# Where the MLP norms' sums of squares are taken in a two-layer hybrid trunk: one-column TensorE products, or ScalarE rows of the turned residual

## Chip, cores and metric

The kernel runs on one core of a Trainium2 chip. The metric is the device time of one execution in microseconds (us); the time given is the median of three runs. TensorE is called PE below, VectorE DVE, ScalarE ACT, GpSimd POOL, and the DMA queue's engine SP.

## What is computed

The reference is a trunk of two layers over 512 positions with 1024 channels. Each layer is a token mixer (layer 0 a gated DeltaNet, layer 1 a Conformer convolution), a cross-attention of 4 heads into 256 memory rows, and an MLP with 4096 hidden channels. Each of them stands behind an RMS norm and adds onto the residual; a last RMS norm closes.

```python
def rms_norm(x, g):
    y = x * lax.rsqrt(jnp.mean(x * x, axis=-1, keepdims=True) + 1e-6)
    return y * g

def sq_relu_mlp(h, w_up, w_down):
    return jnp.square(jax.nn.relu(h @ w_up)) @ w_down

for layer in range(2):
    h = h + mixer[layer](rms_norm(h, ...))
    h = h + memory_cross_attention(rms_norm(h, xa_norm[layer]), rms_norm(mem, ...), ...)
    h = h + sq_relu_mlp(rms_norm(h, mlp_norm[layer]), mlp_w_up[layer], mlp_w_down[layer])
return rms_norm(h, final_norm)
```

## The kernel before

The residual is held with its channels on the partitions: 8 tiles of 128 channels by 512 tokens (`hres`, in the trace `h`). Every product is made in split precision: each operand is a high part and a low part, and `mm3` (L338 to L342) issues three matmuls for each pair of tiles, `wh` by `xh`, `wh` by `xl` and `wl` by `xh`. Weights come from memory as `raw`; ACT casts `raw` to `wh` (L317), and DVE, for some POOL, subtracts to get `wl` (the helper `tt`, L75). Both subtractions and many other two-input operations therefore show as L75, and are told apart by their tiles.

A `Norm` object collects a norm. `add` is `parts` and `square`: `parts` makes `xh` (ACT, L425) and `xl` (DVE, L78) from the residual tile times the gain; `square` squares the tile on ACT (L447) and adds it to an accumulator, on POOL for all but the last tile and on DVE for the last. `stat` (L454) turns the accumulator into one number for each token: four matmuls of one column each (L458; each a 128 by 128 piece of the squares times a column of ones, and as the operands are 32-bit floats each shows as two records) into the PSUM bank `ssq`, a square root on ACT (L460, behind the load of the table that holds it) and a reciprocal on DVE (L462). For the MLP, `stat(rb2)` squares that reciprocal once more (L464): the MLP's input is not scaled by the norm's factor at all, and since the squared ReLU turns a factor r into r squared, its output is multiplied by `rb2` when it is taken.

The cross-attention's output projection ends in `o_ev` (L1056), which for each of 8 tiles adds the residual (DVE) and calls `nxt.add`, where `nxt` is the MLP's norm. The seven-product forms of the input (`seven`, L430, called for X_FORMS) need four DVE sums on the tiles `ua` and `ub` and two casts and two subtractions (`x41h`, `x23h`, `x41l`, `x23l`) for each pair of tiles.

`mlp` (L1105) runs through four groups of 1024 hidden channels. A group has four pairs p, each of an even and an odd tile (`up_even`, `up_odd`). Group 0 makes its 8 up-products with 24 matmuls each; after each of these 8, `first_chunk(n)` (L1271) hangs in side work: `stat(rb2)` after product 1; after the products 0, 1, 2 and 3 the turning of the residual of one block of 128 tokens (`turn_in`, for each half of the channels 4 PE transposes into the PSUM bank `rT` and an ACT copy to `y`); the last `seven` after product 0. For each pair, ACT casts the squared ReLU to `bh`, DVE makes `bl`, then the sums for the seven-product form and their splits `s41h`, `s41l`, `s23h`, `s23l`.

The down-projection of a group is made by seven products in the order M1, M5, M6, M3, M7, M2, M4 (`product`, L1201, matmuls at L1220 to L1222). M5 goes into two banks `dnc`; its first half uses the pairs p = 0 and 1, its second half p = 2 and 3, and needs `s41h` and `s41l` of these pairs. `take` (L1224, DVE) multiplies a bank by `rb2` and adds it to `y`. At the end of layer 0, `stat_tokens` (L472) makes the next norm's factor from sums of squares that ACT took with its accumulator (L1253); at the end of layer 1, `early` and `late` (L1228 to L1243) do the same for the last norm, block by block: square with accumulator, square root, reciprocal, two scalings and the DMAs out.

The program is written for a tile scheduler: it gives every tile a buffer in a pool (68 in the pool of 512-wide tiles, 8 PSUM banks), sets the semaphores, and decides from its own estimates the order in which each engine's instructions stand. So a change of a few lines moves others.

Of the kernel before, what the change touches and what calls it, by code (L numbers as in the profile page):

```python
# [10 lines left out]
AF = mybir.ActivationFunctionType  # L11
ALU = mybir.AluOpType
# [6 lines left out]
EPS = 1e-6  # L19
# [19 lines left out]
def tile_trunk(ctx, tc, xT, memT, prm_d, adt_d, bdw_d, tap_d, fin_d, w_ab, w_kq, w_v, w_z, w_dno, w_pw1, w_pw2,  # L39
               w_q, w_k, w_vv, w_o, w_up, w_dn, yT):  # L40
    nc = tc.nc
    pe, act, dve, pool = nc.tensor, nc.scalar, nc.vector, nc.gpsimd
# [9 lines left out]
    def nm(s):  # L52
        cnt[0] += 1
        return f"{s}_{cnt[0]}"

    def slot(dt=F32, s="u", shape=(P, NT)):
        return up.tile(list(shape), dt, tag="u", name=nm(s))
# [7 lines left out]
    def psum(s="ps"):  # L65
        return psp.tile([P, NT], F32, tag="ps", name=nm(s))

    def small(n, s="sm"):
        return sp.tile([P, n], F32, tag="sm", name=nm(s))
# [4 lines left out]
    def tt(e, o, a, b, op):  # L74
        return e.tensor_tensor(out=o, in0=a, in1=b, op=op)  # L75
# [4 lines left out]
    def ts(e, o, a, s1, op0, s2=None, op1=None):  # L80
        if op1 is None:
            e.tensor_scalar(out=o, in0=a, scalar1=s1, scalar2=None, op0=op0)
        else:
            e.tensor_scalar(out=o, in0=a, scalar1=s1, scalar2=s2, op0=op0, op1=op1)

    def c4(t):
        return t.rearrange("p (c i) -> p c i", c=4)

    def over_i(t4, n=P):
        return t4.unsqueeze(2).to_broadcast([P, t4.shape[1], n])  # L90

    def over_c(t, n=4):
        return t.unsqueeze(1).to_broadcast([P, n, t.shape[1]])
# [302 lines left out]
    def diag2(v, n):  # L396

        vh = sp.tile([P, n], F32R, tag="sm", name=nm("vh"))
        dve.tensor_copy(vh, v)
        vl = small(n, "vl")  # L400
        tt(dve, vl, v, vh.bitcast(F32), ALU.subtract)
        r = []
        for x in (vh.bitcast(F32), vl):
            d = slot(F32R, "dg")[:, 0:n * P]
            tt(dve, d.rearrange("p (c i) -> p c i", c=n), over_c(ident, n), over_i(x), ALU.mult)
            r.append(d)
        return r
# [6 lines left out]
    class Norm:  # L414
# [36 lines left out]
            else:  # L451
                tt(dve if self.n == KT else self.eng, self.acc, self.acc, sq, ALU.add)

        def stat(self, squared=None):  # L454
            ps = psum("ssq")
            for c in range(4):
                cs = slice(c * P, (c + 1) * P)
                pe.matmul(ps[:, c:c + 1], self.acc[:, cs], ones[:, 0:1], start=True, stop=True)  # L458
            sd = small(4, "sd")
            act.activation(sd, ps[:, 0:4], AF.Sqrt, bias=eps_rms, scale=1.0 / 1024)  # L460
            self.tok = small(4, "rstd")
            dve.reciprocal(self.tok, sd)  # L462
            if squared is not None:
                tt(dve, squared, self.tok, self.tok, ALU.mult)  # L464
                return
            if self.two:
                self.dg = diag2(self.tok, 4)
                return
            self.dg = slot(s="dg")
            tt(dve, c4(self.dg), over_c(ident), over_i(self.tok), ALU.mult)  # L470
# [19 lines left out]
    def keepc(n, s):  # L490
        return cp.tile([P, n], F32, tag=s, name=s)
# [496 lines left out]
    def xattn(layer, norm, hres, nxt):  # L988
# [67 lines left out]
        def o_ev(m, ps):  # L1056
            hn = slot(s="h")
            if layer == 0:
                tt(dve, by_phase(hn), phased(ps), phased(hres[m]), ALU.add)
            else:  # L1060
                tt(dve, hn, ps, hres[m], ALU.add)
            new.append(hn)
            nxt.add(m, hn)
            for q in range(4):
                if X_FORMS[q] == m - 8:
                    nxt.seven(q, *new[2 * q:2 * q + 2])

        def ow(m):
            return wnext(("xo", layer, m // 2), m % 2), psum("xo")
# [23 lines left out]
        for k in (6, 7):  # L1093
            proj(w0, outs, p0, k, k + 1)
            proj(w1, outs, p1, k, k + 1)
        o_ev(0, p0)
        o_ev(1, p1)
        for m in range(2, 8):
            w, ps = ow(m)
            proj(w, outs, ps)  # L1100
            o_ev(m, ps)
# [2 lines left out]

    def mlp(layer, norm, hres, nxt, mid=None):  # L1105
        xs = norm.xs
        rb2 = keepc(4, f"rb2_{layer}")
        last = layer == 1
        y = [[None] * 2 for _ in range(4)]
        bank, forms, done = {}, {}, {}  # L1110
# [5 lines left out]
        def turn_in(t, half):  # L1116
            ps = psum("rT")
            for j in range(4):
                pe.transpose(ps[:, j * P:(j + 1) * P], hres[4 * half + j][:, t * P:(t + 1) * P], ident)
            y[t][half] = slot(s="y")  # L1120
            act.copy(y[t][half], ps)

        def lows(src, s):
            h, lo = slot(F32R, s + "h"), slot(F32R, s + "l")
            act.copy(h, src)
            tt(dve, lo, src, h.bitcast(F32), ALU.subtract)
            return [(h[:, c], lo[:, c]) for c in (slice(0, 256), slice(256, 512))]
# [141 lines left out]
            nxt.stat_tokens(ss)  # L1269

        def first_chunk(n):  # L1271
            if n == 1:
                norm.stat(rb2)
            for t in range(4):
                if TURN_IN[t] == n:
                    for half in range(2):
                        turn_in(t, half)
            for q in range(4):
                if X_FORMS[q] == n:
                    norm.seven(q, hres[2 * q], hres[2 * q + 1])  # L1280

        new = [None] * 8
        for g in range(4):
            for p in range(4):
                if (g, p) in UP_SEVEN:
                    up_seven(g * 4 + p)
                    continue
                for i in range(2):
                    ps = psum("up")
                    proj(wnext(("up", layer, g * 4 + p), i), xs, ps)  # L1290
                    rest()
                    (up_odd if i else up_even)(p, ps)
                    if g == 0:
                        first_chunk(2 * p + i)
# [39 lines left out]
    def phased(t):  # L1334
        return t.rearrange("p (t s) -> p s t", s=4)

    def by_phase(t):
        return t.rearrange("p (s t) -> p s t", s=4)
# [272 lines left out]
    for gq in range(2):  # L1611
# [17 lines left out]
        n = 0  # L1629
# [52 lines left out]
    h = xattn(0, n1, h, n2)  # L1682
    n3 = Norm("cv_norm", dve)
    h = mlp(0, n2, h, n3, lambda i: mem_gain(1, i - 1) if i else (mem_load(), taps(NTAP)))
    n4 = Norm("xa_norm1")
    h = conformer(n3, h, n4)
    n5 = Norm("mlp_norm1")
    h = xattn(1, n4, h, n5)
    mlp(1, n5, h, None)


# [154 lines left out]
```

## Time and profile before

| | |
|---|---|
| median of three runs | 1486.53 us (1486.28 to 1486.94) |
| the profiled execution's own time | 1486.58 us |
| its span in the trace | 1484.9 us |
| granted PE clock | 0.997 of full speed |
| matmul records, all records of ACT, DVE, POOL | 7852; 1479, 1834, 293 |
| busy time of ACT and POOL | 862.6 us (58%), 335.9 us (23%) |

The profile comes from one execution, and its rows are read like this: start in us, duration in us, engine, line of the kernel, operation, output and inputs, shape, how many in a row; in brackets the idle time of the engine ahead of it and what ended it. Matmuls overlap, so the pace of PE is read from start to start, 0.23 us for a 512-column matmul, and not from the durations. 1.68 us of the execution lie around the span.

### The profile page before, as it was taken

How to read it: one execution, taken by the hardware profiler on the slowest of the kernel's cores; microseconds unless marked ns; L12 is line 12 of the kernel's file. 1: busy time of each engine (PE TensorE's matmuls, PEld its weight loads, DVE VectorE, ACT ScalarE, POOL GpSimd, SP SyncE). 2: the span in 40 equal slices, each digit the busy share in tenths (PEclk: the TensorE clock that was granted, in tenths of full speed). 3: DMA queues.
4: the chain of work that ended last, by engine and by line, in shares of the span. 5: the costliest groups of instructions: out<-in, count | busy, mean ns of one | idle time of the engine just before them, and what ended most of it. 6: DMA issues, size and time to landing. Idle time of an engine off the chain costs nothing. (4 is left out here: it accounts for less than half of the span.)

```text
span 1484.9 us, 21162 instructions
## 1 busy us (share of the span) xinstructions
PE 1465.1 (99%) x7852; PEld 1252.8 (84%) x7852; DVE 1151.9 (78%) x1834; ACT 862.6 (58%) x1479; POOL 335.9 (23%) x293
## 2 busy tenths in 40 slices
PE   9999999999999999999999999999999999999998
PEld 6888888988888888888898888978888888888886
DVE  6898889867555787888879599975547696978787
ACT  6846665655444764646466865364435755646465
POOL 1321120102111302213040357312111304131220
PEclk9999999999999999999999999999999999999999
DMA  5321223552212214142341794643213223231501
GB/s 205 100 86 57 72 86 101 175 179 76 87 66 72 86 38 161 58 138 90 113 159 62 201 241 132 215 155 111 75 43 107 79 85 108 78 128 57 170 29 57
DMA packets 54966, 161.01 MB, mean 108 GB/s; under 512 B 6864, under 2 KB 8656, under 8 KB 54864
## 3 DMA queue, kind: packets, MB, share of 16 engines
q1 hardware_dynamic: 53136, 153.38, 31.4%
q0 software_dynamic: 1728, 6.29, 2.3%
q8 instruction: 62, 1.02, 0.3%
q14 instruction: 40, 0.33, 0.1%
HBM read 156.76 MB, written 2.10 MB: 107 GB/s over the span
## 5 line engine op out<-in xcount | busy, mean ns | idle before, releaser
L317 ACT CAST wh<-raw 128x1024 fp32r<-128x1024 f32 (+1 forms) x340 | 327.3, 975 | 353.3 <-issue 68.1
L75 DVE TENSOR_TENSOR wl<-raw,wh 128x1024 fp32r<-128x1024 f32 (+1 forms) x272 | 320.8, 1190 | 99.8 <-ACT wh L317 98.3
L75 POOL TENSOR_TENSOR wl<-raw,wh 128x1024 fp32r<-128x1024 f32 x68 | 150.2, 2213 | 426.2 <-ACT wh L317 402.9
L340 PE MATMUL up<-xh,wh 128*128 128x512 f32 x320 | 125.4, 392 | 0.0
L341 PE MATMUL up<-xl,wh 128*128 128x512 f32 x320 | 124.9, 390 | 0.5 <-DVE xl L78 0.5
L342 PE MATMUL up<-xh,wl 128*128 128x512 f32 x320 | 124.6, 389 | 0.0
L75 DVE TENSOR_TENSOR raw<-raw,raw 128x512 f32<-128x512 f32 (+1 forms) x120 | 97.6, 825 | 1.3 <-DMA raw<-w_up 0.6
L78 DVE SCALAR_TENSOR_TENSOR ca<-x,prm,ca 128x512 f32<-128x512 f32 x120 | 88.3, 748 | 3.3 <-ACT ca L1431 1.3
L340 PE MATMUL h<-xh,wh 128*128 128x512 f32 x192 | 77.8, 405 | 2.2 <-ACT xh L425 2.2
L341 PE MATMUL h<-xl,wh 128*128 128x512 f32 x192 | 75.9, 395 | 0.1
L342 PE MATMUL h<-xh,wl 128*128 128x512 f32 x192 | 75.8, 395 | 0.0
L341 PEld LDWEIGHTS up<-xl,wh 128*128 128x128 f32 x320 | 60.2, 188 | 12.4 <-DVE xl L78 0.9
L342 PEld LDWEIGHTS up<-xh,wl 128*128 128x128 f32 x320 | 60.1, 188 | 12.5
L75 POOL TENSOR_TENSOR sq<-sq,sq 128x512 f32<-128x512 f32 x24 | 37.4, 1557 | 146.7 <-ACT sq L447 109.1
L340 PEld LDWEIGHTS up<-xh,wh 128*128 128x128 f32 x320 | 60.2, 188 | 11.7
L78 DVE SCALAR_TENSOR_TENSOR cva<-cv,prm,cva 128x512 f32<-128x512 f32 x60 | 49.4, 840 | 12.0 <-POOL cva L75 10.9
L1221 PE MATMUL dnc<-wh,s41l 128*128 128x512 f32 x128 | 50.0, 391 | 0.5 <-DVE s41l L75 0.5
L340 PE MATMUL pw<-xh,wh 128*128 128x512 f32 x128 | 50.2, 392 | 0.0
L340 PE MATMUL q<-xh,wh 128*128 128x512 f32 x128 | 50.1, 392 | 0.0
L341 PE MATMUL xo<-aol,wh 128*128 128x512 f32 x128 | 50.0, 391 | 0.0
L341 PE MATMUL q<-xl,wh 128*128 128x512 f32 x128 | 49.9, 390 | 0.0
L342 PE MATMUL pw<-xh,wl 128*128 128x512 f32 x128 | 49.8, 389 | 0.0
(458 smaller groups left out, 4261.1 us busy)
## 6 DMA issues: line engine op xcount, KB each, us to landing
raw<-w_up SPq DMA_DIRECT2D x64, 512.0 KB, 3.7
raw<-w_dn SPq DMA_DIRECT2D x40, 512.0 KB, 4.5
raw<-w_dn SPq DMA_DIRECT2D x48, 256.0 KB, 3.4
raw<-w_pw SPq DMA_DIRECT2D x24, 512.0 KB, 4.7
raw<-w_kq SPq DMA_DIRECT2D x16, 512.0 KB, 3.9
raw<-w_k SPq DMA_DIRECT2D x16, 512.0 KB, 4.3
raw<-w_vv SPq DMA_DIRECT2D x16, 512.0 KB, 4.5
raw<-w_q SPq DMA_DIRECT2D x16, 512.0 KB, 3.6
```

The lines of the kernel that those rows point to most:

```text
L75: return e.tensor_tensor(out=o, in0=a, in1=b, op=op)
L78: return dve.scalar_tensor_tensor(out=o, in0=a, scalar=s, in1=b, op0=op0, op1=op1)
L317: ins = [act.copy(h_, r), tt(pool if gp else dve, l_, r, h_.bitcast(F32), ALU.subtract)]
L340: pe.matmul(ps, wh, xh, start=first, stop=False)
L341: pe.matmul(ps, wh, xl, start=False, stop=False)
L342: pe.matmul(ps, wl, xh, start=False, stop=last)
L1221: pe.matmul(ps, al[:, cs], w[hf][0][:, s_], start=False, stop=False, skip_group_check=more)
```

## The change

The change touches the norm ahead of each of the two MLPs and nothing else in the source. The cross-attention no longer squares and adds the residual tiles; `stat` loses its `squared` argument, and the MLP doesn't call it. Instead, `turn_in` squares the turned residual right from the PSUM bank on ACT, with the accumulator summing each row of 512 into a column of a new tile `sq8`. A row of the turned bank is a token, so the eight columns hold the two halves of the sum for four blocks of tokens. After the last block (t = 3, product 3), DVE adds the two halves, scales them and adds epsilon, and takes the reciprocal: `rb2` without a square root.

```diff
-        def stat(self, squared=None):
+        def stat(self):
             ps = psum("ssq")
...
             dve.reciprocal(self.tok, sd)
-            if squared is not None:
-                tt(dve, squared, self.tok, self.tok, ALU.mult)
-                return
             if self.two:
...
             new.append(hn)
-            nxt.add(m, hn)
+            nxt.parts(m, hn)
...
-        rb2 = keepc(4, f"rb2_{layer}")
+        rb2, sq8 = keepc(4, f"rb2_{layer}"), keepc(8, f"sq8_{layer}")
...
             act.copy(y[t][half], ps)
+            act.activation(slot(s="fq"), ps, AF.Square, accum_out=sq8[:, 4 * half + t:4 * half + t + 1])
...
         def first_chunk(n):
-            if n == 1:
-                norm.stat(rb2)
             for t in range(4):
                 if TURN_IN[t] == n:
                     for half in range(2):
                         turn_in(t, half)
+                    if t == 3:
+                        tt(dve, rb2, sq8[:, 0:4], sq8[:, 4:8], ALU.add)
+                        ts(dve, rb2, rb2, 1.0 / 1024, ALU.mult, EPS, ALU.add)
+                        dve.reciprocal(rb2, rb2)
```

Counted over the program, for each MLP: PE loses the four `ssq` products (8 records); ACT loses 8 squares from SBUF, the root and one table load and gains 8 squares with accumulator; POOL loses 6 adds; DVE loses one 512-wide add and two operations on 4 columns and gains three such. The number of table loads stays at 26: the root's table is now loaded ahead of the root in `stat_tokens` and, at the end of layer 1, between the first `late` block's square and its root. SP's order is unchanged.

The scheduler also moves instructions that the source doesn't touch. On ACT, in group 0 of layer 0's MLP, the turn-ins of the last two blocks read as follows before (`rT` are the turned banks, `bh` the cast of the second pair):

```order
L1121 COPY y_5097<-rT_5092 128x512
L1121 COPY y_5104<-rT_5099 128x512
L317 CAST wh_5160<-raw_5107 128x1024
L1121 COPY y_5146<-rT_5141 128x512
L1121 COPY y_5153<-rT_5148 128x512
L1144 ACTIVATE up_5106<-up_5106 128x512
L1145 ACTIVATE up_5106<-up_5106 128x512
L1125 CAST bh_5190<-up_5106 128x512
```

And so after the change, on the same engine (three lines less in the source put L1121 at L1118, L1144 at L1142 and L1125 at L1123):

```order
L1118 COPY y_5073<-rT_5068 128x512
L1119 ACTIVATE fq_5075,sq_0_4874<-rT_5068 128x512
L1118 COPY y_5082<-rT_5077 128x512
L1119 ACTIVATE fq_5084,sq_0_4874<-rT_5077 128x512
L1118 COPY y_5126<-rT_5121 128x512
L1119 ACTIVATE fq_5128,sq_0_4874<-rT_5121 128x512
L1118 COPY y_5135<-rT_5130 128x512
L1119 ACTIVATE fq_5137,sq_0_4874<-rT_5130 128x512
L317 CAST wh_5147<-raw_5087 128x1024
L1142 ACTIVATE up_5086<-up_5086 128x512
L1143 ACTIVATE up_5086<-up_5086 128x512
L1123 CAST bh_5177<-up_5086 128x512
```

Four squares now stand ahead of the cast `bh` of the second pair, beside the four of the earlier blocks, and the weight cast has moved behind them.

On DVE, the last pair's `s41l` of the same group, which M5's second half needs, stood before the change as the seventh row here:

```order
L75 TENSOR_TENSOR up_5302<-u_1141_5294,up_5302 128x256
L75 TENSOR_TENSOR wl_5373<-raw_4740,wh_5372 128x1024
L75 TENSOR_TENSOR u_1141_5294<-up_5302,u_1141_5294 128x256
L78 SCALAR_TENSOR_TENSOR y_4948<-dna_5357,rb_0_4896,y_4948 128x512
L75 TENSOR_TENSOR up_5302<-up_5302,u_1141_5294 128x256
L78 SCALAR_TENSOR_TENSOR y_5021<-dna_5364,rb_0_4896,y_5021 128x512
L75 TENSOR_TENSOR s41l_5344<-up_5302,s41h_5343 128x512
```

After the change, the same engine at the same place:

```order
L75 TENSOR_TENSOR wl_5360<-raw_4726,wh_5359 128x1024
L75 TENSOR_TENSOR up_5289<-u_1138_5281,up_5289 128x256
L78 SCALAR_TENSOR_TENSOR y_4926<-dna_5344,rb_0_4873,y_4926 128x512
L75 TENSOR_TENSOR u_1138_5281<-up_5289,u_1138_5281 128x256
L78 SCALAR_TENSOR_TENSOR y_4993<-dna_5351,rb_0_4873,y_4993 128x512
L75 TENSOR_TENSOR up_5289<-up_5289,u_1138_5281 128x256
L75 TENSOR_TENSOR wl_5380<-raw_4781,wh_5379 128x1024
L75 TENSOR_TENSOR wl_5398<-raw_4958,wh_5397 128x1024
L75 TENSOR_TENSOR s41l_5331<-up_5289,s41h_5330 128x512
```

Two 1024-wide subtractions `wl`, which came behind `s41l` before, now stand ahead of it.

On PE, M5's second half (`dnc`) and the beginning of M6 (`dna`, which uses `s23`) stood like this before; the row with `s41l_5344` is the second of the last pair:

```order
L1220 MATMUL dnc_5396<-wh_5351,s41h_5286 128x512
L1221 MATMUL dnc_5396<-wh_5351,s41l_5287 128x512
L1222 MATMUL dnc_5396<-wl_5352,s41h_5286 128x512
L1220 MATMUL dnc_5396<-wh_5351,s41h_5343 128x512
L1221 MATMUL dnc_5396<-wh_5351,s41l_5344 128x512
L1222 MATMUL dnc_5396<-wl_5352,s41h_5343 128x512
```

After the change, on PE from the seventh matmul of M5's second half (the six ahead of it are the third pair's, for both banks):

```order
L1218 MATMUL dna_5344<-wh_5359,s23h_5056 128x512
L1218 MATMUL dnc_5383<-wh_5338,s41h_5330 128x512
L1218 MATMUL dnc_5390<-wh_5338,s41h_5330 128x512
L1219 MATMUL dna_5344<-wh_5359,s23l_5057 128x512
L1220 MATMUL dna_5344<-wl_5360,s23h_5056 128x512
L1218 MATMUL dna_5344<-wh_5359,s23h_5190 128x512
L1219 MATMUL dna_5344<-wh_5359,s23l_5191 128x512
L1220 MATMUL dna_5344<-wl_5360,s23h_5190 128x512
L1219 MATMUL dnc_5383<-wh_5338,s41l_5331 128x512
```

The last pair's `s41l` is wanted after 4 matmuls of this half before, and after 14 now: the third pair's products for the second bank and six matmuls of M6 have moved ahead of it.

## The prediction

> **What bounds the kernel now.** I read the page first, then PE's list of waits, then the timelines of PE, DVE, POOL and ACT around the places that the change touches. The page's line of busy times:
>
> ```profile
> PE 1465.1 (99%) x7852; PEld 1252.8 (84%) x7852; DVE 1151.9 (78%) x1834; ACT 862.6 (58%) x1479; POOL 335.9 (23%) x293
> ```
>
> PE is busy for 99% of the span, so a step matters only where it adds to PE's stream, takes from it, or makes PE wait. Two of PE's waits lie in the two MLPs and can be reached by this change. The first is in layer 0, at the end of the first up-product; PE waits for the last tile's `xl`:
>
> ```profile
> 498.01 0.39 PE L340 MATMUL up<-xh,wh 128*128 128x512 f32 x1
> 498.86 0.50 PE L341 MATMUL up<-xl,wh 128*128 128x512 f32 x1 [0.46 <-DVE xl L78]
> 499.20 0.40 PE L342 MATMUL up<-xh,wl 128*128 128x512 f32 x1
> ```
>
> The matmuls start 0.85 and 0.34 us apart in place of 0.23 each, the pace of such matmuls (rows 1161.19 and 1161.42 below): 0.73 us are lost. The other wait comes in both MLPs, in M5's second half of group 0, where PE wants `s41l` of the last pair:
>
> ```profile
> 550.56 0.39 PE L1222 MATMUL dnc<-wl,s41h 128*128 128x512 f32 x1
> 550.97 0.49 PE L1220 MATMUL dnc<-wh,s41h 128*128 128x512 f32 x1
> 551.69 0.50 PE L1221 MATMUL dnc<-wh,s41l 128*128 128x512 f32 x1 [0.23 <-DVE s41l L75]
> 552.03 0.39 PE L1222 MATMUL dnc<-wl,s41h 128*128 128x512 f32 x1
> ```
>
> ```profile
> 1207.32 0.50 PE L1221 MATMUL dnc<-wh,s41l 128*128 128x512 f32 x1 [0.22 <-DVE s41l L75]
> ```
>
> From 550.56 to 552.03 are 1.47 us for three steps of 0.23, so 0.78 us are lost; layer 1 shows the same wait. This place I call the meeting point: here PE has caught up with the chain ACT to DVE. What PE gains ahead of it is kept only if this chain becomes no later.
>
> **What PE is spared.** The one-column products stand in PE's stream like this, layer 0 and layer 1, each with the transposes behind them:
>
> ```profile
> 505.77 0.95 PE L458 MATMUL ssq<-ones,sq 128*128 128x1 f32 x8
> 506.57 0.42 PE L1119 MATMUL rT<-ident,h 128*128 128x128 f32 x2
> ```
>
> ```profile
> 1161.19 0.39 PE L342 MATMUL up<-xh,wl 128*128 128x512 f32 x1
> 1161.42 0.95 PE L458 MATMUL ssq<-ones,sq 128*128 128x1 f32 x8
> 1162.23 0.64 PE L1119 MATMUL rT<-ident,h 128*128 128x128 f32 x4
> ```
>
> From start to start that is 0.80 and 0.81 us. They go. The wait for `xl` goes too, I think, through POOL. One row of POOL and two of DVE:
>
> ```profile
> 495.77 1.29 POOL L75 TENSOR_TENSOR sq<-sq,sq 128x512 f32<-128x512 f32 x1 [8.64 <-ACT sq L447]
> ```
>
> ```profile
> 495.84 2.31 DVE L75 TENSOR_TENSOR wl<-raw,wh 128x1024 fp32r<-128x1024 f32 x1
> 498.07 0.74 DVE L78 SCALAR_TENSOR_TENSOR xl<-h,prm,xh 128x512 fp32r<-128x512 f32 x1
> ```
>
> POOL's last add of squares ends at 497.06, and the subtraction that DVE began under it takes 2.31 us, where the same operation takes 1.22 alone (the group's mean, quoted below). Without squares to add, POOL isn't there, `wl` ends 1.09 earlier, and `xl` about as much, ahead of the 498.24 at which PE wants it: 0.73 gained. So ahead of the meeting point PE gains 0.80 + 0.73 = 1.53 us in layer 0 and 0.81 in layer 1, 2.34 in all.
>
> **What ACT gets in return.** A square with accumulator is shown elsewhere in the same program, on the same shape, from SBUF:
>
> ```profile
> 1462.13 0.64 ACT L1230 ACTIVATE fq<-y 128x512 f32<-128x512 f32 x1
> 1462.67 0.19 ACT L1230 ACTIVATION_READ_ACCUMULATOR fq<-y 128x1 f32 x1
> 1462.79 0.63 ACT L1230 ACTIVATE fq<-y 128x512 f32<-128x512 f32 x1
> ```
>
> Start to start 0.66 us; if nothing overlapped it would be 0.64 + 0.19 = 0.83. No square from PSUM is shown, so 0.66 to 0.83 are my bounds, and I take 0.66, as the instructions of ACT here also stand close. Eight make 5.3 us, inside the first half of group 0, where ACT leads DVE and DVE leads PE. The squares that go lay in the cross-attention, where ACT waits for residual tiles, and free nothing here. These are ACT's rows of before in that stretch, with POOL's of the same time:
>
> ```profile
> 503.31 0.62 ACT L377 CAST x41h<-ub 128x512 fp32r<-128x512 f32 x1 [2.38 <-DVE ub L75]
> 506.37 1.09 ACT L1121 COPY y<-rT 128x512 f32<-128x512 f32 x2
> 508.56 1.07 ACT L317 CAST wh<-raw 128x1024 fp32r<-128x1024 f32 x1
> 509.65 1.28 ACT L460 ACT_TABLE_LOAD   x1
> 510.94 0.26 ACT L460 ACTIVATE sd<-ssq,eps_rms 128x4 f32<-128x4 f32 x1
> 512.71 0.62 ACT L377 CAST x41h<-ub 128x512 fp32r<-128x512 f32 x1 [1.50 <-DVE rstd L462]
> 513.23 0.58 ACT L1144 ACTIVATE up<-up 128x512 f32<-128x512 f32 x1
> ```
>
> ```profile
> 500.53 2.40 POOL L75 TENSOR_TENSOR wl<-raw,wh 128x1024 fp32r<-128x1024 f32 x1 [3.47 <-PE rT L1119]
> 509.70 2.61 POOL L75 TENSOR_TENSOR wl<-raw,wh 128x1024 fp32r<-128x1024 f32 x1 [6.78 <-ACT wh L317]
> ```
>
> And DVE's, of which the first goes and the second is the sum that `x41h` at 503.31 waits for:
>
> ```profile
> 498.73 0.68 DVE L75 TENSOR_TENSOR sq<-sq,sq 128x512 f32<-128x512 f32 x1
> 500.70 2.51 DVE L75 TENSOR_TENSOR ub<-ub,ua 128x256 f32<-128x256 f32 x1
> ```
>
> Step by step. Without the slow `wl` and the add, DVE starts its four sums 1.7 us earlier; they then end before POOL's `wl` at 500.53, under which the last of them took 2.51 us. So `x41h` comes at about 499.2, four us earlier. ACT can't keep all of that, as it waits for the first pair's `al`; I put the first turn-in copy at 503.7, 2.7 earlier than 506.37. Two squares (1.3) follow, and the cast of 508.56 ends 1.4 earlier. POOL's `wl` of 509.70 waits for this cast, blocks DVE's next sum for its 2.6 us, and now ends 1.4 earlier; `x41h` of 512.71, which needs this sum, is 1.4 earlier. (Its row names `rstd`, since that stood last on DVE ahead of it; the load and `sd` are no longer in ACT's way.) The two activations of the next tile (L1144, L1145), at 0.5 each from start to start, now stand ahead of `x41h` and fill its wait: 1.0 earlier. Then six squares come before the second pair's `bh`: 4.0 later. Together +1.6 us for this row:
>
> ```profile
> 525.42 0.59 ACT L1125 CAST bh<-up 128x512 fp32r<-128x512 f32 x1
> ```
>
> Bounds: without the head start of 1.4 it is +3.0; with 0.83 for each of six squares 1.0 more; at the other end, if all of the 2.7 came through, 1.3 less, +0.3.
>
> `rb2` costs nothing: it's wanted at the first `take`, and on DVE behind its add stands only `bl` of the second pair, which waits for that same `bh`.
>
> **The meeting point.** From that pair's `bl` to `s41l` of the last pair DVE has little slack; the stretch in layer 0 and in layer 1, then two groups of the first:
>
> ```profile
> 526.04:550.95 24.91, 23.53 (x36) 1.00 0.06 21
> 1181.67:1206.59 24.92, 23.54 (x36) 1.00 0.06 22
> ```
>
> ```profile
> L75 DVE TENSOR_TENSOR wl<-raw,wh 128x1024 fp32r<-128x1024 f32 x5 | 6.1, 1220 | 0.4 <-ACT wh L317 0.4
> L75 DVE TENSOR_TENSOR s41l<-up,s41h 128x512 fp32r<-128x512 f32 x3 | 2.1, 688 | 0.7 <-ACT s41h L1125 0.7
> ```
>
> Only 1.38 of 24.91 us are idle, 1.1 of it waiting for ACT (0.7 for `s41h`, 0.4 for `wh`). After the change two more `wl` stand ahead of the last `s41l`. What a pair costs:
>
> ```profile
> 552.15 2.35 DVE L75 TENSOR_TENSOR wl<-raw,wh 128x1024 fp32r<-128x1024 f32 x2
> 554.42 0.74 DVE L78 SCALAR_TENSOR_TENSOR y<-dnc,rb,y 128x512 f32<-128x512 f32 x1
> ```
>
> That is 2.27 us. With `wl` and `raw` work now standing ahead of the `s41l` that waited for ACT, I let the 1.1 us of idle be used up (bounds: none, or all 1.38). The last `s41l` comes 1.6 + 2.3 - 1.1 = 2.8 us later. PE, however, wants it ten matmuls later, 10 x 0.227 = 2.3 us. Net: PE leaves the meeting point 0.5 us later than before, in each MLP, whatever it gained on the way. What it gained it waits: the wait grows from 0.78 lost to about 0.8 + 1.5 + 0.5 = 2.8 in layer 0, and 2.1 in layer 1. Twice 0.5 is +1.0.
>
> **The two moved table loads.** A load now stands ahead of this root, at the end of layer 0:
>
> ```profile
> 828.11 0.28 ACT L475 ACTIVATE sd<-ms,eps_rms 128x4 f32<-128x4 f32 x1
> ```
>
> The root is 1.28 late, but the factor it makes isn't wanted by the next product, which runs on unscaled `xh` tiles made behind it; I take 0.1, bounds 0 and 0.5. The other stands between the first `late` block's square and root, before this row of the last block:
>
> ```profile
> 1478.82 0.63 ACT L1237 ACTIVATE fq<-y 128x512 f32<-128x512 f32 x1 [0.73 <-DVE y L78]
> ```
>
> ACT still waits 0.73 for DVE's `y` in the last block, and waits earlier in the tail too, so most of 1.28 is absorbed; I take 0.2 at the end, bounds 0 and 0.5.
>
> A rule weighed against a row: the load at 509.65 lasts 1.28 and `sd` follows at 510.94, 0.01 us after its end, and the cast ahead of it ends at 509.63. The Trainium skill (ScalarE: Activation LUTs, section What ACT_TABLE_LOAD costs) gives about 1.28 us for the load and a drain of about 1.38 besides, 2.66 for every switch. This trace agrees on the first and shows no drain; by the page's sum the tail's row would be up to 1.4 later, and the estimate for the time 1.4 higher.
>
> **The sum.** The profiled execution took 1486.58 us, 0.05 above the median of 1486.53, so I use it as it is: 1486.58 + 1.0 + 0.1 + 0.2 = **1487.9 us**. About 0.2%, 3.0 us, is what a measurement of this kernel can tell from no change, so faster is below 1483.6 and slower above 1489.5.
>
> **Rivals.**
>
> The cover holds (faster or same). `s41l` comes early enough that PE doesn't lose more than before at the meeting point: 1486.58 - 2.34 + 0.3 = 1484.5; if the wait there vanishes as well, 2 x 0.78 less, 1483.0. For it speaks that ACT is busy only 58% of the whole. Against it: the stretch's 1.38 us of idle can't take two `wl` and a late `bh`. It needs `bh` to be no later than before. Chance 0.14, half of it at 1484.5 (same), half at 1483.0 (faster).
>
> ACT's head start doesn't come (slower). If POOL's `wl` of 509.70 keeps its time, because ACT waits for the first pair's `al` until 506 as before, `bh` is 3.0 late instead of 1.6, and each MLP loses 1.4 more: 1487.9 + 2.8 = 1490.7. For it: layer 1 has no wait for `xl`, so its sums may be less changed than layer 0's. Against: the load and `sd` left ACT either way. It decides from 0.8 us of these 1.4. Chance 0.17.
>
> The load drains (a rule of its own, the skill's of above): a load in the tail keeps ACT 2.66 us, and 1.38 of these come on top, 1489.3. Against it stands the row at 510.94. Chance 0.03.
>
> That the change doesn't do what it says: the wait at 498.86 stays, as `xl` then waits for something else on DVE. It would change nothing, since PE waits at the meeting point anyway; it is inside the forecast.
>
> **How the numbers follow.** The forecast has 0.66 and lies within 0.2%. Faster: 0.07. Slower: 0.17. Same: 0.66 + 0.07 + 0.03 = 0.76. The range goes from 1484.5, the cover that holds but for the old wait, to 1490.7, the missing head start; between them lie the bounds of the single costs (idle not absorbed: 2 x 1.1 more, 1490.1). Outside are the vanished wait, 0.07, and a part of the slower rival where costs add up, about 0.08.
>
> **What would show it.** Right: no `ssq` in either MLP and no wait for `xl` at the first up-product; 0.8 us less between PE's products there; `bh` of the second pair 1.6 us later and `s41l` of the last pair 2.8 later than before; at M5's second half PE loses over 2 us in place of 0.78, in both layers; ACT's squares with accumulator 0.66 apart. Wrong: a meeting point without a longer wait (then the time is below 1485), a `bh` 3 us late, or a wait of PE in a place that has none now, such as the fifth up-product's bank, or the start of layer 1's products behind the moved load.

## The result, and the profile after

The changed kernel takes **1482.65 us** (median of 13 runs, 1481.49 to 1484.39) against 1485.91 us for the kernel before beside it (13 runs, 1485.47 to 1488.48). The medians are 3.26 us apart; the ratio of the runs is 0.9975, with a 95% interval of 0.9967 to 0.9982, that is 2.7 to 4.9 us less. The forecast was 1487.9 us, no difference that can be measured, with a range down to 1484.5; the time lies below it. The profiled execution took 1482.22 us, with a span of 1480.4.

The page's line of busy times after the change:

```profile
PE 1461.6 (99%) x7836; PEld 1250.9 (84%) x7836; DVE 1140.3 (77%) x1834; ACT 862.2 (58%) x1493; POOL 318.0 (21%) x281
```

PE has 3.5 us less to do or to stretch over, POOL 17.9 less, ACT the same: what it gave up and what it took on are alike in sum. Where the time went is read by laying the same matmul of both traces side by side, from place to place; the difference changes at these places only:

| place | PE's difference, after less before |
|---|---|
| start to the first MLP (nothing changed there) | -0.37 us |
| layer 0, last `xl` of the first up-product | -0.74 |
| layer 0, one-column products | -0.78 |
| layer 0, M5's second half, together with M6 | -0.32 |
| layer 1, a wait in the convolution | -0.72 |
| layer 1, one-column products | -0.77 |
| layer 1, M5's second half | -0.67 |
| tail | 0.0 to -0.1 |

The places that the change touches sum to 3.28 us, about the 3.26 between the medians. The first row and the convolution's are matters of the executions that were profiled. For the first row, the granted PE clock is 0.50 over the stretch from 8.0 to 14.6 us in the profile before and over that from 8.7 to 11.9 after, and behind it PE is 1.1 us ahead; a wait of 0.8 us in the mixer, for ACT's `w`, which the profile before doesn't have, takes 0.7 of them back. Other profiles show the same wait at 0.3 to 0.9 us or not at all, before the change and after it. In the convolution PE waits for a row that waits for a weight's transfer. In the kernel before, PE's list of waits, and the row on ACT that came late:

```profile
PE lnT L1499 <- DVE cy L84: 1.2, 1, 1.2
```

```profile
967.35 1.05 ACT L317 CAST wh<-raw 128x1024 fp32r<-128x1024 f32 x1 [0.63 <-DMA raw<-w_vv]
```

After the change this cast follows at once and the wait is 0.5. Of the twelve runs below, one shows 1.5 and the others 0.5, and no row of the convolution stands elsewhere after the change, so I don't count it.

PE at the end of the first up-product of layer 0, and at the end of its second, after the change:

```profile
497.64 0.39 PE L340 MATMUL up<-xh,wh 128*128 128x512 f32 x1
497.86 0.39 PE L341 MATMUL up<-xl,wh 128*128 128x512 f32 x1
498.09 0.40 PE L342 MATMUL up<-xh,wl 128*128 128x512 f32 x1
498.32 1.04 PE L1116 MATMUL rT<-ident,h 128*128 128x128 f32 x8
...
504.45 0.39 PE L342 MATMUL up<-xh,wl 128*128 128x512 f32 x1
504.68 1.03 PE L1116 MATMUL rT<-ident,h 128*128 128x128 f32 x8
```

The matmuls start 0.23 us apart to the last, and the transposes follow the second product with no `ssq` between. Both gains came as forecast. The meeting point did not. PE in M5's second half, layer 0 and then layer 1:

```profile
551.27 0.40 PE L1220 MATMUL dna<-wl,s23h 128*128 128x512 f32 x1
551.76 0.50 PE L1219 MATMUL dnc<-wh,s41l 128*128 128x512 f32 x1
552.10 0.39 PE L1220 MATMUL dnc<-wl,s41h 128*128 128x512 f32 x1
```

```profile
1205.08 0.40 PE L1220 MATMUL dna<-wl,s23h 128*128 128x512 f32 x1
1205.31 0.39 PE L1219 MATMUL dnc<-wh,s41l 128*128 128x512 f32 x1
```

In layer 0, two steps of 0.49 and 0.34 where 0.23 is normal: 0.37 us lost, before 0.78 and by the forecast 2.8. In layer 1 PE meets `s41l` without any wait. The prediction had named this as a sign that it was wrong: a meeting point without a longer wait, with a time below 1485.

### The profile page after: what moved, and what is told of

Same layout as the page of the kernel before. It is cut to its first block, busy times and chain, and to the rows that moved or that the text cites. A ratio compares the mean times of both kernels' runs of the same rounds, so it can differ in the third digit from the quotient of the medians.

```text
span 1480.4 us, 21122 instructions
## 1 busy us (share of the span) xinstructions
PE 1461.6 (99%) x7836; PEld 1250.9 (84%) x7836; DVE 1140.3 (77%) x1834; ACT 862.2 (58%) x1493; POOL 318.0 (21%) x281
## 5 line engine op out<-in xcount | busy, mean ns | idle before, releaser
L342 PE MATMUL q<-xh,wl 128*128 128x512 f32 x128 | 49.9, 390 | 0.0
```

The costliest lines, as they stand in the source:

```text
L342: pe.matmul(ps, wl, xh, start=False, stop=last)
```

## The experiments

Two questions are open: is it the meeting of the chain ACT to DVE with PE at M5 that sets what a step is worth, as the forecast had it, and why was the chain not later? All times are medians; the kernel before had 1486.37 us beside the first four, 1486.31 beside the others. As the kernel before thus differs by up to 0.5 us from set to set (1485.91 beside the changed kernel), a difference of a microsecond between medians of two sets says little; differences by place are read from the profiles, as in the table above.

**No squares.** In `turn_in` the square goes; `sq8` is filled with a constant at the start of `mlp`, so the MLP norm's factor is left out.

```diff
-            act.activation(slot(s="fq"), ps, AF.Square, accum_out=sq8[...])
+        dve.memset(sq8, 512.0)
```

> The changed kernel without its eight squares for each MLP (sq8 is filled with a constant, so the norm's factor in the MLP is left out). Theory 1, the meeting point decides: the chain ACT to DVE and PE come together at M5's second half, and in the changed kernel they meet almost exactly (0.4 us of wait in layer 0, under 0.1 in layer 1). Without squares the chain is about 4 us earlier and nothing but this wait is left to gain: 0.3 to 0.6 us less than the changed kernel, 3.6 to 3.9 less than before. Theory 2, the squares hold up PE or its banks elsewhere in group 0 too: 1.5 us or more less than the changed kernel.

Measured: 1481.46 us, ratio to before 0.9967 (0.9955 to 0.998). By place, 0.5 us less than the changed kernel at M5 in layer 0 and 0.14 in layer 1, and 0.1 or less elsewhere. The eight squares, 4.6 us of ACT in each MLP, cost PE 0.6 to 0.7 us in all.

**Squares twice.**

```diff
             act.activation(slot(s="fq"), ps, AF.Square, accum_out=sq8[...])
+            act.activation(slot(s="fq"), ps, AF.Square, accum_out=sq8[...])
```

> The changed kernel with every square of a turned bank taken twice. Measured price of one square with accumulator from PSUM: 0.58 us from start to start; six more stand ahead of the second pair's bh, 3.5 us. Theory 1, the meeting point decides: PE wants the last s41l only a matmul earlier than in the changed kernel, so each MLP loses 2.5 to 3.5 us there: 5 to 7 us more than the changed kernel, some 2 to 4 slower than before. Theory 2, ACT has slack here (58% busy) and squares are free: within 0.5 us of the changed kernel.

Measured: 1492.35 us, ratio 1.0038 (1.0026 to 1.0051): 9.7 more than the changed kernel. ACT's time isn't free, but the size and the place were missed. PE loses 4.9 us in each MLP, in layer 0 4.1 of them by the first third of the fifth up-product, whose bank was the first pair's odd tile and comes free with its `s41l`. PE at the end of the wait, and then PE's windows, one before it and two behind it:

```profile
521.88 0.50 PE L340 MATMUL up<-xh,wh 128*128 128x512 f32 x1 [2.28 <-DVE s41l L75]
```

```profile
512.00:518.50 6.50, 6.50 (x34) 1.00 0.14 52
523.00:526.20 3.20, 3.20 (x9) 0.50 0.74 252
526.40:530.00 3.60, 3.60 (x18) 1.00 0.02 9
```

The number behind the bracket is the granted clock, the one in it counts the matmuls. A wait of 2.3 us is followed, about 1 us later, by 3.2 us at half the clock, 9 matmuls where 14 would fit: the wait is paid once more by two thirds. The forecast of this run had the late chain wait at M5; it waits at the fifth product first, and 0.7 us are lost at M5.

**M6 held behind M5.** On PE alone, the order that the scheduler chose is undone in part; `ins` is M6's first matmul for each of its banks.

```diff
+                    if g == 0 and name == "M6" and step[0] == 0 and kk == 0:
+                        tc.keep_in_program_order(ins)
```

> The changed kernel with M6's first product of group 0 held behind the last matmul of M5, in both MLPs; nothing else moves, on ACT and DVE the order is the same. PE then wants the last pair's s41l after 8 matmuls of M5's second half and not after 14: 6 x 0.227 = 1.4 us sooner. Theory 1, the meeting point decides: the wait there grows by 1.4 us in layer 0 and about 1.3 in layer 1, 2.7 us more than the changed kernel, 0.6 less than before. Theory 2, the order of these matmuls is of no account, since the chain is early enough: within 0.5 us of the changed kernel.

Measured: 1484.92 us, ratio 0.9991 (0.9982 to 0.9999): 2.3 more than the changed kernel, and by place 1.4 in each layer. PE in layer 0:

```profile
549.84 0.73 PE L1218 MATMUL dnc<-wh,s41h 128*128 128x512 f32 x2
551.83 0.50 PE L1221 MATMUL dnc<-wh,s41l 128*128 128x512 f32 x1 [1.25 <-DVE s41l L75]
```

`s41l` comes when it came, PE stands there six matmuls sooner, and waits just these. The meeting point decides, and most of the gain, 2.8 of 3.28 us, needs the new order at M5.

**The kernel before with one square.** Only the first residual tile is squared; POOL's adds and the last one on DVE go, while the one-column products, the root and the load stay. Seven eighths of the sum of squares are left out.

```diff
-            nxt.add(m, hn)
+            nxt.parts(m, hn)
+            if m == 0:
+                nxt.square(hn)
```

> The kernel before with the square of the first residual tile alone (of the sum of squares seven eighths are left out): no adds on POOL and none on DVE, but the one-column products, the root and the table load stay. Theory 1: the wait for xl goes (0.73), and as DVE's sums no longer meet POOL the chain reaches M5 over 2 us earlier, so that both waits there go (1.55): about 2.3 us less than before, 1 more than the changed kernel. Theory 3, POOL's adds are of no account and the whole gain is the one-column products and the load: within 0.8 us of before. Theory 4, POOL's adds are the whole: 3.3 us less than before.

Measured: 1483.69 us, ratio 0.9982 (0.9973 to 0.9991), 2.7 less than before. By place: the wait for `xl` 0.74, M5 0.80 in layer 0 and 0.73 in layer 1, 2.27 together, as forecast by the theory of the meeting point. The chain is so early here that M5 in program order meets no wait.

**The kernel before without the one-column products,** the root and the load (`rb2` is a constant, which leaves the norm's factor out); squares and adds stay.

```diff
             if n == 1:
-                norm.stat(rb2)
+                dve.memset(rb2, 1.0)
```

> The kernel before without the one-column products, the root and the table load of the MLP (rb2 is filled with a constant, so the norm's factor in the MLP is left out); the squares and POOL's adds in the cross-attention stay. Theory 1, the meeting point decides: the chain to the last s41l isn't touched, since its x41h waits for DVE's sum under POOL's wl and not for the load, so the 0.8 us that PE is spared in each MLP only lengthen its wait at M5: within 0.5 us of before. Theory 3, the products are PE's time outright: 1.6 us less than before; with the wait gone as well, 3 less.

Measured: 1485.09 us, ratio 0.9994 (0.9985 to 1.0003), which doesn't tell it from before. By place, 0.85 goes with the products in each layer and 0.32 comes back at M5 at once; another 0.28 comes back late in layer 1's MLP, where PE waits for a sum on DVE. The 0.8 of gain in all lies between the theories: the chain is a little earlier without root and load, but not by as much as PE.

**Four one-column products put back** into the changed kernel, without a use.

```diff
+            if n == 1:
+                ps = psum("ssq")
+                for c in range(4):
+                    pe.matmul(ps[:, c:c + 1], hres[0][:, c * P:(c + 1) * P], ones[:, 0:1], start=True, stop=True)
```

> The changed kernel with four one-column products after the second up-product of each MLP (of a residual tile, into a bank that nobody reads). They cost PE 0.8 us. Theory 1: PE waits 0.4 us at M5 in layer 0 and next to nothing in layer 1, so 0.4 of the first is hidden: 1.2 us more than the changed kernel. Rival, PE's stream ahead of M5 is of no account, as the meeting point alone sets the time: within 0.3 us of the changed kernel.

Measured: 1483.43 us, ratio 0.9981 (0.9972 to 0.999), 0.8 more than the changed kernel. By place 0.84 in each layer, of which 0.4 is given back in layer 0, where the wait at M5 goes, and nothing in layer 1: 1.3 in all, as theory 1 had it. Where the chain is in time, PE's stream is worth its full length.

**The old squares and adds kept** in the changed kernel, their sum unused.

```diff
-            nxt.parts(m, hn)
+            nxt.add(m, hn)
```

> The changed kernel with the old squares and adds in the cross-attention kept besides, their sum unused: POOL's adds are back, ACT's squares of the changed kernel stay. Theory 1: the wait for xl returns (0.7), DVE's sums meet POOL again, so the chain to the last s41l loses its head start of over 2 us, and as M5's order goes back by some matmuls too, PE waits 2 to 4 us more in each MLP: 4 to 8 us more than the changed kernel, slower than before by 1 to 5. This would be the sum that was forecast for the change itself. Theory 3, POOL's adds are of no account: within 0.8 us of the changed kernel.

Measured: 1490.01 us, ratio 1.0027 (1.0017 to 1.0038), 7.4 more than the changed kernel and slower than before. In layer 0 by place: `xl` 0.76, the fifth product's bank 1.8, M5 and the rows ahead of it 1.2. PE's two new waits there:

```profile
520.70 0.50 PE L340 MATMUL up<-xh,wh 128*128 128x512 f32 x1 [1.53 <-DVE s41l L75]
...
552.93 0.73 PE L1218 MATMUL dnc<-wh,s41h 128*128 128x512 f32 x2 [1.07 <-ACT s41h L1123]
```

This is the condition of the slower rival of the forecast, made real: without the head start the second pair's `bh` comes 3.5 us later than before, against PE's own start of the MLP (that rival had 3.0). The time is near that rival's 1490.7 too, but in part by luck: over half of what PE loses, 1.8 us in each layer, it loses at the fifth product's bank and not at M5, and the wait for `xl` is back besides.

**Turn-ins spread out,** after the products 0, 2, 4 and 6.

```diff
-TURN_IN = (0,1,2,3)
+TURN_IN = (0,2,4,6)
```

> The changed kernel with the four turn-ins after the products 0, 2, 4 and 6 of group 0 and not after 0, 1, 2 and 3, which spreads the squares. Theory 1: four squares and four copies leave the way of the second pair's bh, the chain is earlier, and the last wait at M5 goes: 0.5 us less than the changed kernel, and nothing more is to be had there. Theory 2, squares cost in other places too (banks held by the turned tiles): 1.5 us less, or more where they now fall.

Measured: 1485.19 us, ratio 0.9994 (0.9985 to 1.0003), 2.5 more than the changed kernel where I expected half a microsecond less. The second pair's `bl` is earlier indeed (521.40 where 525.76 stood), but the last squares now run from 541.90 to 543.67 on ACT, ahead of the last pair, whose `bl` comes at 548.09 and not at 544.50. PE in layer 0:

```profile
552.97 0.74 PE L1218 MATMUL dnc<-wh,s41h 128*128 128x512 f32 x2 [1.73 <-ACT s41h L1123]
```

The waiting row now wants `s41h`. Squares nearer to the meeting point have less time to be caught up.

**The kernel before with its adds on DVE.** No work is left out or added; six adds in each cross-attention change the engine.

```diff
-    n2 = Norm("mlp_norm0")
+    n2 = Norm("mlp_norm0", dve)
```

(and the same for the other layer)

> The kernel before with the six adds of squares of each cross-attention on DVE in place of POOL; no other row moves to another engine. If POOL's adds hurt by running beside DVE, the wl ahead of the last xl takes 1.2 us and not 2.3, and the wait for xl shrinks or goes; the adds cost DVE 6 x 0.6 us, but it has idle time in the cross-attention. Theory 1: 0.5 to 1.5 us less than before, without the one-column products' 1.6. Rival, it is the adds themselves, on whatever engine, that hold up the chain: no gain, or up to 1 us more than before.

Measured: 1484.27 us, ratio 0.9987 (0.9978 to 0.9996), 2.0 less than before. The subtraction ahead of the last `xl`, on DVE:

```profile
495.16 1.22 DVE L75 TENSOR_TENSOR wl<-raw,wh 128x1024 fp32r<-128x1024 f32 x1
```

1.22 us where it took 2.31 beside POOL's add. By place, 0.44 is gained at `xl` and 0.8 at M5 in each layer; 0.7 is lost from the end of layer 0 to the convolution, whose wait is the one of 1.5 us. So at `xl` it was POOL's add running beside DVE, not the adding, that held DVE up. At M5 this run doesn't show that the adds alone did it, since the scheduler moved a row here too: ACT's weight cast for POOL stands behind the table load (508.11, load 506.66), so POOL's second `wl` starts at 509.23, and DVE's second sum, at 508.05, is through ahead of it in 0.43 us, where the one at 510.10 took 2.50 under POOL's `wl` before. What holds the chain up most is thus a sum on DVE under a weight subtraction on POOL. In this run it is the second such sum that escapes in layer 0; with POOL's adds gone, in the run with one square and after the change, it is the first.

**The last turn-in after the fifth product,** `TURN_IN = (0,1,2,4)`.

> The changed kernel with the last of the four turn-ins after the fifth up-product of group 0 and not after the fourth. Two copies and two squares, 2.1 us, leave the way of the second pair's bh and come ahead of the third pair's, where ACT has over 1 us to spare; in PE's order M5 is now taken in program order, so PE wants the last s41l ten matmuls, 2.3 us, sooner than in the changed kernel. Theory 1: the two balance, and as the wait for s41l at M5 in layer 0 (0.4) may go or stay: from 0.6 less to 0.5 more than the changed kernel. Rival, as in the run with the turn-ins spread wider, squares that come later hit the last pair: 2 us more or worse.

Measured: 1483.72 us, ratio 0.9981 (0.9973 to 0.999). By place nothing changes in sum: 0.0 in layer 0, 0.0 in layer 1. The last `s41l` is earlier by 2.3 us, which is what PE, now in program order at M5, wants it sooner. The median is 1.1 more than the changed kernel's all the same, with runs from 1480.72 to 1485.48. Its profile loses 1.4 us against the first profile of the changed kernel in the first 25 us of the program, where the granted clock is 0.50 from 20.9 to 24.2, behind a wait of 1.0 us and a stretch of one-column products; whether the other executions lost it there too isn't known.

**Squares read from the copy in SBUF,** `y[t][half]` in place of `ps`.

> The changed kernel with each square read from the copy y in SBUF and not from the bank. Each then waits for the end of the copy ahead of it on ACT where nothing stands between; if that is 0.15 us for eight squares, bh of the second pair comes up to 1 us later, and PE loses that at M5: up to 2 us more than the changed kernel in the two MLPs. Rival: the wait is hidden, as the scheduler puts other rows between: within 0.3 us of the changed kernel.

Measured: 1483.86 us, ratio 0.9984 (0.9975 to 0.9993), 1.2 more than the changed kernel; by place 0.76 and 0.74 at M5. A copy and its square take 1.26 us from SBUF (copies at 501.53 and 502.79) and 1.06 from the bank (502.56 and 503.62).

**The changed kernel again.**

> The changed kernel once more, beside the three others on the same chip, as the mark for them. By the places that the two traces differ in: 3.3 us less than before; the waits for s41l at M5 0.4 us in layer 0 and under 0.1 in layer 1; the wait in the convolution for cy, which stood at 1.2 us in the one profile of before and at 0.5 in the others, 0.5.

Measured: 1482.66 us, ratio 0.9978 (0.9969 to 0.9987); PE's difference to the first profile of the changed kernel is 0.3 to 0.5 us all along, and the convolution's wait is 0.5.

None of the complete kernels beats the changed one.

## Why the forecast was wrong, point by point

**What PE is spared** was right: 0.74, 0.78 and 0.77 us where 0.73, 0.80 and 0.81 stood, and the reason given for `xl` is shown by the run with the adds on DVE. These are DVE's rows after the change:

```profile
494.35 1.21 DVE L75 TENSOR_TENSOR wl<-raw,wh 128x1024 fp32r<-128x1024 f32 x1
495.49 0.73 DVE L78 SCALAR_TENSOR_TENSOR xl<-h,prm,xh 128x512 fp32r<-128x512 f32 x1
```

**The meeting point** exists and decides, as the run with M6 held behind M5 shows, and the one with one square from the other side, where the chain is earlier and both waits go. Squares twice and adds kept show a chain that is late; PE then pays most of it earlier, at the fifth product's bank. PE does want the last `s41l` ten matmuls later. The step that failed is the sum "The last `s41l` comes 1.6 + 2.3 - 1.1 = 2.8 us later". Taken against PE's own start of the MLP (0.37 earlier in this trace, 2.95 in layer 1), it came 0.44 us later in layer 0 and 0.80 in layer 1. Less the 2.27 of the ten matmuls, PE is 1.83 and 1.47 earlier behind the meeting point, and the places in the table give 1.84 and 1.44. Both halves of the sum were too large.

The first term, 1.6 for the second pair's `bh`, measured 0.1 in layer 0 and 0.5 in layer 1. The head start that was forecast for ACT is there: DVE's last sum for the first `x41h` took 2.51 us under POOL's `wl` before, and now it is through ahead of it.

```profile
497.88 0.42 DVE L75 TENSOR_TENSOR ub<-ub,ua 128x256 f32<-128x256 f32 x1
```

ACT after the change, layer 0, and POOL's row behind the cast at 505.89:

```profile
498.40 0.62 ACT L377 CAST x41h<-ub 128x512 fp32r<-128x512 f32 x1 [1.92 <-DVE ub L75]
...
502.56 0.61 ACT L1118 COPY y<-rT 128x512 f32<-128x512 f32 x1
503.04 0.63 ACT L1119 ACTIVATE fq<-rT 128x512 f32<-128x512 f32 x1
503.53 0.22 ACT L1119 ACTIVATION_READ_ACCUMULATOR fq<-rT 128x1 f32 x1
503.62 0.61 ACT L1118 COPY y<-rT 128x512 f32<-128x512 f32 x1
...
505.89 1.08 ACT L317 CAST wh<-raw 128x1024 fp32r<-128x1024 f32 x1
...
509.99 0.62 ACT L377 CAST x41h<-ub 128x512 fp32r<-128x512 f32 x1 [1.91 <-DVE ub L75]
...
525.14 0.59 ACT L1123 CAST bh<-up 128x512 fp32r<-128x512 f32 x1
```

```profile
507.05 2.62 POOL L75 TENSOR_TENSOR wl<-raw,wh 128x1024 fp32r<-128x1024 f32 x1 [3.29 <-ACT wh L317]
```

From the square's start to the next row's, 503.04 to 503.62, are 0.58 us, not the 0.66 that a square from SBUF took behind another: six make 3.5 and not 4.0. And more of the head start came through: I let ACT spend over a microsecond of it waiting for the first pair's `al`, and put the first copy 2.7 earlier than before; against PE's start it is 3.4 earlier. Everything behind follows by the links that were named: the cast 2.3 earlier, POOL's `wl` as much, the second `x41h` 2.35 where I took 1.4. Then -2.35 - 1.0 + 3.5 = 0.15, about the 0.1 that is measured. My lower bound for this term was 0.3; I chose nearer to the middle without a row for it.

The second and third terms, 2.3 less 1.1, measured 0.35: DVE's stretch from the second pair's `bl` to the last `s41l`, its window and its ends.

```profile
525.76:551.02 25.26, 25.00 (x38) 1.00 0.06 21
```

```profile
525.76 0.69 DVE L75 TENSOR_TENSOR bl<-up,bh 128x512 fp32r<-128x512 f32 x1 [2.08 <-ACT bh L1123]
...
551.02 0.68 DVE L75 TENSOR_TENSOR s41l<-up,s41h 128x512 fp32r<-128x512 f32 x1
```

Two more subtractions, 2.27 us, fit into 0.35. The idle time fell from 1.38 to 0.26 us, about as I allowed. The other 0.8 is time that no row shows as idle. Of it, 0.3 lies at the three waits for ACT: their rows show 1.10 us as idle, but from start to start they cost 1.39, since a row that had to wait doesn't overlap the row ahead of it. The other 0.5 lies between the rows. Before the change and after it, DVE's sums of one pair:

```profile
526.84 0.43 DVE L75 TENSOR_TENSOR up<-u,up 128x256 f32<-128x256 f32 x1
527.30 0.42 DVE L75 TENSOR_TENSOR u<-up,u 128x256 f32<-128x256 f32 x1
```

```profile
528.50 0.42 DVE L75 TENSOR_TENSOR up<-up,u 128x256 f32<-128x256 f32 x1
528.83 1.22 DVE L75 TENSOR_TENSOR raw<-raw,raw 128x1024 f32<-128x1024 f32 x1
```

In these rows, one that reads what the row ahead of it writes starts 0.46 us after it, one that doesn't 0.33. The scheduler put `wl` and `raw` between the dependent rows, and so found room for a part of the work that I added at full price.

Since the chain was 2.4 us earlier than I had it in layer 0 (2.0 in layer 1), PE kept what it had gained. The single parts tell the same: POOL's adds gone and PE's products still there gives 2.3 by place, the products gone and the adds still there 0.8; both, with the squares paid for, 3.3.

**The moved table loads** cost nothing that shows, where I had 0.1 and 0.2. In the tail of the changed kernel, ACT:

```profile
1468.18 0.19 ACT L1235 ACTIVATION_READ_ACCUMULATOR fq<-y 128x1 f32 x1
1468.38 1.28 ACT L1236 ACT_TABLE_LOAD   x1
1469.68 0.29 ACT L1236 ACTIVATE sm<-sm,fb 128x1 f32<-128x1 f32 x1
...
1475.63 0.72 ACT L1238 ACTIVATE y<-y,sm 128x512 f32<-128x512 f32 x1 [0.23 <-DVE sm L1237]
```

The last row stands 4.47 us earlier than before, as PE's last products do (4.4). The load takes 1.28 us and the root follows 0.02 after it; the drain of about 1.38 us that the Trainium skill gives besides (ScalarE: Activation LUTs, What ACT_TABLE_LOAD costs) isn't in this trace either, and the measurement decides.

**The rivals.** What happened is the one called "the cover holds", to which I gave 0.14; with 0.4 us of wait left it came between its two times, by the places of the change 1486.58 - 3.28 = 1483.3. That the measured median, 1482.65, lies below both is a matter of the start: the forecast counted from 1486.58, the profiled execution, and the kernel before beside the changed one has a median of 1485.91. The argument against this rival, that it needed a `bh` no later than before and that the stretch behind it couldn't take two subtractions, fails: `bh` was 0.1 and 0.5 us later, the stretch took the two for 0.35, and the ten matmuls covered the sum.

## What to carry to other kernels

Where two engines meet, cost a change on both sides of the meeting: what the engine that waits is spared is kept only as far as the chain that it waits for is no later than it is wanted, and taking POOL's work from beside DVE can advance that chain by about as much as the moved work delays it. In a chain of short rows on one engine, ask what the scheduler can put between dependent rows before adding new work at full price. And when a term has bounds far apart, and several such terms add up, don't take the dear half of each.

## What the runs showed of the hardware that was not expected

- POOL and DVE, both on operands in SBUF: the same 1024-wide subtraction on DVE takes 1.21 or 1.22 us alone and 2.31 when it starts under POOL's add (ends at 497.06, with `xl` at 498.07 behind it). The Trainium skill (SBUF — State Buffer, Who interferes with whom) says that a DVE operation with two inputs in SBUF contends with a GpSimd operation that reads SBUF; the run that moved the adds to DVE agrees (1.22). A sum of 128x256 took 0.42 us alone and 2.51 under POOL's `wl`.
- In the run with the squares twice, a wait of 2.28 us on PE, behind eight transposes, was followed about 1 us later by 3.2 us at half the clock (granted 0.50, matmuls 0.43 us apart), and so was one of 1.85 in layer 1; the waits of 1.73 and 1.53 in other runs show nothing of the kind. No least wait follows from this: near the start of the program, in this run and in the one with the last turn-in after the fifth product, the granted clock is 0.50 for 3.3 us behind a wait of 1.0 us and one-column products.
- A square with accumulator costs ACT 0.58 us from a PSUM bank between copies and 0.66 from SBUF; in one stretch of the kernel the copy and the square took 1.06 and 1.26 us together.
